# Mixture-of-experts layer: x in two loads of four experts, and the last weight but one in a single load

## The chip, the core and the metric

The kernel runs on one core of a Trainium2 chip. The metric is the device time of one execution in microseconds (us), as the median of five runs. A profile of one execution stands beside it.

## What is computed

Eight experts each have 256 rows of x, a first weight and a second weight; all inputs and the output are float32.

```python
# x: (8, 256, 512)   w1: (8, 512, 2048)   w2: (8, 2048, 512)
h = np.matmul(x, w1)
h = np.maximum(h, 0)
return np.matmul(h, w2).astype(np.float32)
```

Each w1[e] and each w2[e] is 4.19 MB in float32, so the sixteen weights are 67.1 MB; x is 4.19 MB and the output 4.19 MB.

## The kernel before

The matrix products run in bfloat16. The weights are loaded by GpSimd's DMA queue, which casts float32 to bfloat16 on the way; a weight tile holds 2048 KB after the cast, with 16 KB (32 KB before the cast) in each of the 128 partitions. `w1` and `w2` tiles each have three buffers (`WB = 3`), so `load_w1(3)` may start only when expert 0's first layer has read its weight, and so on. The queue works in the order of issue, and the order of the program is written out by hand (`manual_schedule`).

`first_layer(e)` makes the hidden layer of one expert: 16 blocks of 128 hidden units, each from four matmuls that contract over the 512 inputs, 64 matmuls of 128x256 in all. Four blocks share a PSUM tile, and ScalarE and VectorE take turns to apply relu and write `ht` as bfloat16. `second_layer(e)` makes 32 matmuls of 128x512, which alternate between the two row blocks and go through the 16 row groups (kt) of w2 in order; VectorE copies one result to `o_sb` and ScalarE the other.

x must have its inputs on the partitions, so it is transposed on TensorE (`transpose_x`, line 87), eight 128x128 blocks to a PSUM tile, and copied from there to `xt` by VectorE (line 100) or ScalarE (line 98). x comes in groups (`GROUPS`): experts 0 and 1 each by a float32 transfer of SyncE into `x_f`, cast by ScalarE (lines 155 and 156); experts 2 and 3 by one casting transfer of GpSimd, and experts 4 to 7 by another (line 65), in the midst of the weights. In `x_rows`, a group of n experts gives each partition 2n rows of 2 KB that lie one after the other in memory: 4 KB for one expert, 8 KB for two, 16 KB for four. The transposes of experts 1 and 2-3 stand between layers; those of experts 4-7 between the parts of `first_layer(2)`.

At the end the order is different: the first layers of experts 5, 6 and 7 run ahead of the second layers of 5, 6 and 7. The second weight of expert 6 comes in two halves of 8 row groups, that of expert 7 in 9 and 7, so that a second layer can start on the first piece (`load_w2`, lines 71 to 75). The results of experts 0 to 4 are stored by GpSimd's queue behind the last weight (`store(0, 5)`); those of expert 5 by five SyncE transfers (lines 191 and 192) while the last weight still arrives; those of experts 6 and 7 by a last SyncE transfer (line 194).

Of the kernel before, what the change touches and what calls it, by code (L numbers as in the profile page):

```python
# [10 lines left out]
def kernel(  # L11
# [7 lines left out]
    nc = tc.nc  # L19
    P = 128  # L20
    bf = mybir.dt.bfloat16
    f32 = mybir.dt.float32
    relu = mybir.ActivationFunctionType.Relu

    E, C, H = x.shape
    F = w1.shape[2]
    MT = C // P
    KT1 = H // P
    KT2 = F // P
# [1 line left out]
    WB = 3  # L31


    GROUPS = ((0, 1), (1, 1), (2, 2), (4, 4))


    w1_r = w1.rearrange("e (p kt) n -> e p kt n", p=P)
# [3 lines left out]
    const = ctx.enter_context(tc.tile_pool(name="const", bufs=1))  # L41
# [7 lines left out]

    w1_sb, w2_sb, ht = {}, {}, {}  # L50
    group_of = {e: g for g, (e0, n) in enumerate(GROUPS) for e in range(e0, e0 + n)}
    x_f = const.tile([P, 2, MT, H], f32, name="x_f")
    x_b = [const.tile([P, n * MT, H], bf, name=f"x_b{g}") for g, (_, n) in enumerate(GROUPS)]
    xt = [const.tile([P, KT1, MT, n * P], bf, name=f"xt{g}") for g, (_, n) in enumerate(GROUPS)]
    o_sb = const.tile([P, E, MT, H], f32, name="out_sb")
    identity = const.tile([P, P], bf, name="identity")

    def x_rows(g):
        e0, n = GROUPS[g]
        return x[e0:e0 + n].rearrange("e c k -> (e c) k").rearrange(  # L60
            "(p j) k -> p j k", p=P
        )

    def load_x(g):
        nc.gpsimd.dma_start(x_b[g][:], x_rows(g))  # L65

    def load_w1(e):
        w1_sb[e] = wpool.tile([P, KT1, F], bf, tag="w1", name="w1_sb")
        nc.gpsimd.dma_start(w1_sb[e][:], w1_r[e])  # L69

    def load_w2(e):
        w2_sb[e] = wpool.tile([P, KT2, H], bf, tag="w2", name="w2_sb")
        cuts = {E - 2: (0, 8, 16), E - 1: (0, 9, 16)}.get(e, (0, KT2))
        for lo, hi in zip(cuts, cuts[1:]):
            nc.gpsimd.dma_start(w2_sb[e][:, lo:hi, :], w2_r[e, :, lo:hi, :])  # L75

    def transpose_x(g, blocks=None):


        n = GROUPS[g][1]  # L80
        J = n * MT
        KB = 8 // J
        for b in blocks if blocks is not None else range(KT1 // KB):
            pt = ps_o.tile([P, KB, J, P], bf, tag="ps_o", name="pt_tr")
            for i in range(KB):
                for j in range(J):
                    nc.tensor.transpose(  # L87
                        pt[:, i, j, :], x_b[g][:, j, b * KB + i::KT1], identity[:]
                    )
            for i in range(KB) if n > 1 else (slice(0, KB),):  # L90
                if n > 1:
                    src = pt[:, i].rearrange("p (l m) q -> p l m q", m=MT)
                    dst = xt[g][:, b * KB + i].rearrange("p m (q l) -> p l m q", l=n)
                    flip = b * KB + i
                else:
                    src, dst, flip = pt[:, i], xt[g][:], g
                if flip % 2:
                    nc.scalar.copy(dst, src)  # L98
                else:
                    nc.vector.tensor_copy(dst, src)  # L100

    def first_layer(e, between=()):
        g = group_of[e]
        i0 = (e - GROUPS[g][0]) * P
        ht[e] = hpool.tile([P, KT2, C], bf, tag="ht", name="ht_sb")
        for q in range(KT2 // FB):
            ph = ps_h.tile([P, FB, C], f32, tag="ps_h", name="pt_h")
            for i in range(FB):
                for kt in range(KT1):
                    nc.tensor.matmul(  # L110
                        ph[:, i, :],
                        w1_sb[e][:, kt, FB * q + i::KT2],
                        xt[g][:, kt, :, i0:i0 + P],
                        start=(kt == 0),
                        stop=(kt == KT1 - 1),
                    )
            if q % 2:
                nc.vector.tensor_relu(ht[e][:, FB * q:FB * (q + 1), :], ph[:])  # L118
            else:
                nc.scalar.activation(ht[e][:, FB * q:FB * (q + 1), :], ph[:], relu)  # L120
            if between:
                between.pop(0)()

    def second_layer(e):
        po = [
            ps_o.tile([P, H], f32, tag="ps_o", name=f"pt_o{mt}") for mt in range(MT)
        ]
        for kt in range(KT2):
            for mt in range(MT):
                nc.tensor.matmul(  # L130
                    po[mt][:],
                    ht[e][:, kt, mt * P:(mt + 1) * P],
                    w2_sb[e][:, kt, :],
                    start=(kt == 0),
                    stop=(kt == KT2 - 1),
                )
        nc.vector.tensor_copy(o_sb[:, e, 0, :], po[0][:])  # L137
        nc.scalar.copy(o_sb[:, e, 1, :], po[1][:])  # L138
# [2 lines left out]
        nc.gpsimd.dma_start(out_r[:, e0:e1], o_sb[:, e0:e1])  # L141


    for e in (0, 1):
        nc.sync.dma_start(x_f[:, e], x_rows(e))
    load_w1(0)
    make_identity(nc, identity)
    load_w2(0)
    load_x(2)
    load_w1(1)  # L150
    load_w2(1)
    load_x(3)
    load_w1(2)
    load_w2(2)
    nc.scalar.copy(x_b[0][:], x_f[:, 0])  # L155
    nc.scalar.copy(x_b[1][:], x_f[:, 1])  # L156
    transpose_x(0)

    first_layer(0)
    load_w1(3)  # L160
    transpose_x(1)
    second_layer(0)
    load_w2(3)
    first_layer(1)
    load_w1(4)
    transpose_x(2)
    second_layer(1)
    load_w2(4)
    first_layer(2, [lambda kt=kt: transpose_x(3, [kt]) for kt in range(KT1)])
    load_w1(5)  # L170
    second_layer(2)
    first_layer(3)
# [52 lines left out]
```

## Time and profile before

| | us |
|---|---|
| median of five runs | 181.71 (181.46 to 181.98) |
| the profiled execution's own time | 181.98 |
| its span, first to last instruction | 180.2 |
| TensorE matmuls busy | 129.2 |
| VectorE busy | 31.8 |
| ScalarE busy | 31.6 |
| GpSimd busy | 12.3 |

The DMA queues moved 40.47 MB as they are counted at the destination, at a mean of 225 GB/s; HBM was read for 71.30 MB and written for 4.19 MB, 419 GB/s over the span. A casting load counts its 2 bytes per value at the destination and reads 4, so a stretch of pure weight loading shows about half the GB/s of a stretch of float32 stores at the same read or write rate. In the row of DMA shares, 9 means that the 16 DMA engines were busy for 90% or more of that fortieth of the span (4.5 us). PE is TensorE, DVE is VectorE, ACT is ScalarE, POOL is GpSimd, SP is SyncE; L130 is line 130 of the kernel.

### The profile page before, as it was taken

To read this page: it belongs to the slowest core of one execution; us is meant where nothing else is said; L and a number is where in the kernel's file an instruction comes from. 1 tells how busy PE (TensorE), PEld (TensorE's weight loads), DVE (VectorE), ACT (ScalarE), POOL (GpSimd) and SP (SyncE) were. 2 spreads that over 40 slices of the span, in tenths; PEclk is the share of its full clock that TensorE was granted. 3 is DMA by queue.
4 is the path that set the end of the run, shared out by engine and by line. 5 is a ranking of instruction groups with operands and counts; after the bars stand their busy time and mean duration, and the time that the engine had idled before them with its cause. 6 is when DMAs were issued, how large, how long until landed. Compare 5 with 4: busy or idle time off the path is not lost.

```text
span 180.2 us, 1823 instructions
## 1 busy us (share of the span) xinstructions
PE 129.2 (72%) x825; PEld 89.8 (50%) x832; DVE 31.8 (18%) x29; ACT 31.6 (18%) x32; POOL 12.3 (7%) x27
## 2 busy tenths in 40 slices
PE   0206999059993199988769794979494967999650
PEld 0105974048841189638624691349394953444220
DVE  0100220101411017610500122012222140011010
ACT  3300240102221026612200230012122220011010
POOL 7300010100101000100100004030000000000000
PEclk9999999956999759999969998799999996999995
DMA  5998999999899999989998999999899999999995
GB/s 220 246 233 185 222 233 211 196 233 225 182 233 233 211 196 233 229 185 225 233 225 182 233 229 204 207 233 225 185 229 233 211 196 211 226 209 223 312 416 230
DMA packets 4262, 40.47 MB, mean 225 GB/s; under 512 B 416, under 2 KB 416, under 8 KB 1952
## 3 DMA queue, kind: packets, MB, share of 16 engines
q0 software_dynamic: 3536, 37.75, 95.7%
q1 hardware_dynamic: 720, 2.62, 3.8%
q8 instruction: 6, 0.10, 0.2%
HBM read 71.30 MB, written 4.19 MB: 419 GB/s over the span
## 4 chain that ended last, share of the span: by engine, by line
DMA 44%; PE 41%; another core or an unknown queue 8%; issue 1%; POOL 1%; ACT 0%; POOLq 0%
DMA w_sb<-in_w_dram 44%; PE pt_o L130 21%; PE pt_h L110 19%; PE pt_tr L87 2%; ACT out_sb L138 0%; POOL x_b L65 0%; POOL w_sb L75 0%; POOL identity masks.py:199 0%; POOL identity masks.py:197 0%; POOL w_sb L69 0%; POOLq L209 0%
## 5 line engine op out<-in xcount | busy, mean ns | idle before, releaser
L110 PE MATMUL pt_h<-xt,w_sb 128*128 128x256 bf16 x512 | 64.9, 292 | 29.8 <-DMA w_sb<-in_w_dram 29.8
L110 PEld LDWEIGHTS <-w_sb 128*128 128x128 bf16 x512 | 59.5, 147 | 35.8 <-DMA w_sb<-in_w_dram 33.0
L130 PE MATMUL pt_o<-w_sb,ht_sb 128*128 128x512 bf16 x249 | 60.6, 400 | 9.7 <-DMA w_sb<-in_w_dram 8.9
L130 PEld LDWEIGHTS <-ht_sb 128*128 128x128 bf16 x256 | 26.0, 102 | 42.4 <-issue 16.0
L118 DVE TENSOR_SCALAR ht_sb<-pt_h 128x1024 bf16<-128x1024 f32 x16 | 19.7, 1228 | 64.6 <-PE pt_h L110 64.6
L120 ACT ACTIVATE ht_sb<-pt_h 128x1024 bf16<-128x1024 f32 x16 | 16.5, 1029 | 67.6 <-PE pt_h L110 67.6
L138 ACT COPY out_sb<-pt_o 128x512 f32<-128x512 f32 x8 | 4.7, 585 | 65.1 <-PE pt_o L130 65.1
L137 DVE COPY out_sb<-pt_o 128x512 f32<-128x512 f32 x8 | 5.5, 692 | 59.8 <-PE pt_o L130 59.8
L100 DVE COPY xt<-pt_tr 128x1024 bf16<-128x1024 bf16 (+1 forms) x5 | 7.1, 1439 | 18.1 <-PE pt_tr L87 18.1
L69 POOL DMA_DIRECT2D w_sb<-in_w_dram x8 | 4.4, 554 | 85.8 <-PE pt_h L110 85.0
L87 PE MATMUL pt_tr<-identity,x_b 128*128 128x128 bf16 x64 | 5.6, 243 | 5.1 <-ACT x_b L155 5.1
L98 ACT COPY xt<-pt_tr 128x1024 bf16<-128x1024 bf16 (+1 forms) x5 | 7.4, 1498 | 7.1 <-PE pt_tr L87 4.5
L87 PEld LDWEIGHTS <-x_b 128*128 128x128 bf16 x64 | 5.0, 122 | 5.2 <-ACT x_b L155 5.1
L75 POOL DMA_DIRECT2D w_sb<-in_w_dram x10 | 5.4, 547 | 23.3 <-PE pt_o L130 23.3
L155 ACT ACT_TABLE_LOAD x1 | 1.3, 1283 | 0.7 <-PEq L209 0.7
L155 ACT CAST x_b<-x_f 128x1024 bf16<-128x1024 f32 x1 | 1.0, 1045 | 2.0 <-DMA x_f<-in_x_dram 2.0
L65 POOL DMA_DIRECT2D x_b<-in_x_dram x2 | 1.1, 552 | 0.0
L156 ACT CAST x_b<-x_f 128x1024 bf16<-128x1024 f32 x1 | 1.0, 1046 | 0.2 <-DMA x_f<-in_x_dram 0.2
L141 POOL DMA_DIRECT2D out_dram<-out_sb x1 | 0.9, 866 | 0.1
masks.py:199 POOL TENSOR_SCALAR_AFFINE_SELECT identity<-identity 128x128 bf16<-128x128 bf16 x1 | 0.3, 288 | 0.1
masks.py:197 POOL MEMSET identity<- 128x128 bf16 x1 | 0.2, 223 | 0.0
L209 POOL MEMSET const-float32-0.0<- 128x1 f32 x1 | 0.1, 98 | 0.2 <-issue 0.2
(3 smaller groups left out, 0.3 us busy)
## 6 DMA issues: line engine op xcount, KB each, us to landing
w_sb<-in_w_dram POOLq DMA_DIRECT2D x14, 2048.0 KB, 45.2
out_dram<-out_sb POOLq DMA_DIRECT2D x1, 2560.0 KB, 55.8
w_sb<-in_w_dram POOLq DMA_DIRECT2D x2, 1024.0 KB, 46.9
w_sb<-in_w_dram POOLq DMA_DIRECT2D x1, 1152.0 KB, 45.2
x_f<-in_x_dram SPq DMA_DIRECT2D x2, 512.0 KB, 3.7
x_b<-in_x_dram POOLq DMA_DIRECT2D x1, 1024.0 KB, 47.9
out_dram<-out_sb SPq DMA_DIRECT2D x1, 1024.0 KB, 4.9
w_sb<-in_w_dram POOLq DMA_DIRECT2D x1, 896.0 KB, 50.2
```

What stands on the lines that cost most here:

```text
L69: nc.gpsimd.dma_start(w1_sb[e][:], w1_r[e])
L75: nc.gpsimd.dma_start(w2_sb[e][:, lo:hi, :], w2_r[e, :, lo:hi, :])
L87: nc.tensor.transpose(pt[:, i, j, :], x_b[g][:, j, b * KB + i::KT1], identity[:])
L98: nc.scalar.copy(dst, src)
L100: nc.vector.tensor_copy(dst, src)
L110: nc.tensor.matmul(ph[:, i, :], w1_sb[e][:, kt, FB * q + i::KT2], xt[g][:, kt, :, i0:i0 + P], start=(kt == 0), stop=(kt == KT1 - 1),)
L118: nc.vector.tensor_relu(ht[e][:, FB * q:FB * (q + 1), :], ph[:])
L120: nc.scalar.activation(ht[e][:, FB * q:FB * (q + 1), :], ph[:], relu)
L130: nc.tensor.matmul(po[mt][:], ht[e][:, kt, mt * P:(mt + 1) * P], w2_sb[e][:, kt, :], start=(kt == 0), stop=(kt == KT2 - 1),)
L137: nc.vector.tensor_copy(o_sb[:, e, 0, :], po[0][:])
L138: nc.scalar.copy(o_sb[:, e, 1, :], po[1][:])
L155: nc.scalar.copy(x_b[0][:], x_f[:, 0])
```

## The change

x now comes in two groups of four experts. The first is one float32 transfer of SyncE (2 MB, 16 KB in each partition), issued before the first weight; VectorE and ScalarE cast it in four pieces, two each, and all of its 32 transposes stand ahead of `first_layer(0)`. The second group is the same as the last of the four groups before. The casting transfer for experts 2 and 3 is gone, and the transposes of experts 1 and 2-3 no longer stand between layers. The second weight of expert 6 comes in one transfer; that of expert 7 is still cut.

```diff
-    GROUPS = ((0, 1), (1, 1), (2, 2), (4, 4))
+    GROUPS = ((0, 4), (4, 4))
...
-    x_f = const.tile([P, 2, MT, H], f32, name="x_f")
+    x_f = const.tile([P, 4 * MT, H], f32, name="x_f")
...
-        cuts = {E - 2: (0, 8, 16), E - 1: (0, 9, 16)}.get(e, (0, KT2))
+        cuts = (0, 9, 16) if e == E - 1 else (0, KT2)
...
-    for e in (0, 1):
-        nc.sync.dma_start(x_f[:, e], x_rows(e))
+    nc.sync.dma_start(x_f[:], x_rows(0))
     load_w1(0)
     make_identity(nc, identity)
     load_w2(0)
-    load_x(2)
     load_w1(1)
     load_w2(1)
-    load_x(3)
+    load_x(1)
     load_w1(2)
     load_w2(2)
-    nc.scalar.copy(x_b[0][:], x_f[:, 0])
-    nc.scalar.copy(x_b[1][:], x_f[:, 1])
+    for j in range(0, 4 * MT, 2):
+        if j % 4:
+            nc.scalar.copy(x_b[0][:, j:j + 2], x_f[:, j:j + 2])
+        else:
+            nc.vector.tensor_copy(x_b[0][:, j:j + 2], x_f[:, j:j + 2])
     transpose_x(0)
 
     first_layer(0)
     load_w1(3)
-    transpose_x(1)
     second_layer(0)
     load_w2(3)
     first_layer(1)
     load_w1(4)
-    transpose_x(2)
     second_layer(1)
     load_w2(4)
-    first_layer(2, [lambda kt=kt: transpose_x(3, [kt]) for kt in range(KT1)])
+    first_layer(2, [lambda kt=kt: transpose_x(1, [kt]) for kt in range(KT1)])
```

## The prediction

> **What bounds the kernel now.** I read the slices of the page first, then the chain of waits, the landings of the loads and the end of the span. The page's slices show DMA at eight tenths or more from the second slice to the last but one, while TensorE has gaps everywhere.
>
> ```profile
> PE   0206999059993199988769794979494967999650
> DMA  5998999999899999989998999999899999999995
> ```
>
> TensorE's waits name the loads. In the list of waits, the first line below is eight first layers that each waited for their weight:
>
> ```profile
> PE pt_h L110 <- DMA w_sb<-in_w_dram: 29.8, 8, 8.9
> PE pt_o L130 <- DMA w_sb<-in_w_dram: 8.9, 4, 2.5
> POOL w_sb L69 <- PE pt_h L110: 85.0, 5, 18.8
> ```
>
> The third line is GpSimd waiting for buffers, up to 18.8 us, and yet the DMA engines do not run dry, because loads are issued far ahead: 45.2 us from issue to landing in the median. So the kernel is one stream of transfers, and its length sets the time. Its unit is one weight. In the timeline, layers that wait for a weight start at 81.69, 91.40, 101.05, 110.73, 120.42, 130.16, 139.81 and 149.49: seven weights in 67.80 us, 9.69 each, or 433 GB/s of reading.
>
> The end follows the stream. The chain in order of time closes so:
>
> ```profile
> 165.08 4.06 PE pt_o L130 x18
> 169.14 1.39 another core or an unknown queue
> 170.53 0.04 issue
> 170.57 3.19 PE pt_o L130 x14
> ```
>
> TensorE has 18 matmuls on the first piece of the last weight, waits 1.39 for the second piece (issued 120.3, 50.2 to landing), does 14 more; the copies and the last store (4.9 us) follow. **What shortens the stream shortens the kernel; what delays TensorE costs nothing until 1.39 us are used up at this place.**
>
> **The x loads.** The timeline of GpSimd gives the issues, and the DMA issues the time to landing (last column):
>
> ```profile
> 2.44 0.55 POOL L75 DMA_DIRECT2D w_sb<-in_w_dram  x1
> 2.98 0.54 POOL L65 DMA_DIRECT2D x_b<-in_x_dram  x1
> 3.51 0.55 POOL L69 DMA_DIRECT2D w_sb<-in_w_dram  x1
> ```
> ```profile
> w_sb<-in_w_dram POOLq DMA_DIRECT2D x1, 2048.0 KB, 22.3
> ...
> x_b<-in_x_dram POOLq DMA_DIRECT2D x1, 512.0 KB, 24.3
> ...
> w_sb<-in_w_dram POOLq DMA_DIRECT2D x1, 2048.0 KB, 34.4
> ...
> x_b<-in_x_dram POOLq DMA_DIRECT2D x1, 1024.0 KB, 47.9
> ```
>
> The first second-layer weight lands at 24.74, the load of experts 2-3 (8 KB rows, 1.05 MB read) at 27.28: it takes 2.54. The load of experts 4-7 (16 KB rows, 2.10 MB) is issued at 4.55 and lands at 52.45, behind a weight of 47.53: 4.92. The two float32 loads of SyncE show in the start of the stream; columns are DMA share and GB/s at the end:
>
> ```profile
> 1.50:2.00 0.50, 0.00 (x0) 0.00 (x0) 0.00 (x0) 0.50 (x1) 0.50 (x2) 1.00 0.78 147
> 2.00:2.50 0.50, 0.00 (x0) 0.00 (x0) 0.00 (x0) 0.02 (x1) 0.42 (x3) 1.00 0.43 156
> 3.00:3.50 0.50, 0.00 (x0) 0.00 (x0) 0.00 (x0) 0.00 (x0) 0.50 (x1) 1.00 1.00 410
> ```
>
> Between 2.0 and 2.5 there is a lull, 57% of 0.5 us = 0.29. From 2.5 to 4.5 the rate is 410 to 426, mean 418: 1.05 MB take 2.51. So x of experts 0 to 3 holds the stream for 2.51 + 0.29 + 2.54 = **5.34** before.
>
> After, the same 2.10 MB come in one transfer. Its nearest row is the load of experts 4-7, with the same bytes read and the same 16 KB rows: 4.92. It differs in that it writes float32, so the other bound is the rate of the SyncE loads, 2.10 MB at 418 GB/s = 5.02. The lull may stay (0.29) or go, since a 16 KB row keeps an engine busy four times as long as a 4 KB row; the trace has no such start, and I take half, 0.15. Together 4.92 + 0.15 = 5.07, between 4.92 and 5.31: a **gain of 0.27 (0.03 to 0.42)**. The first weight, 2.4 us later, and everything up to the old place of experts 2-3 move back; behind that place they move forward.
>
> **The second weight of expert 6.** Its halves are issued at 109.61 and 110.15 and land at 154.3 (44.7 later) and 159.25 (49.1, since the two have a median of 46.9); the weight ahead lands at 149.48. So it takes 9.77 in two pieces against 9.69: **gain 0.08 (0 to 0.1)**.
>
> On TensorE this takes cover away. The second layer of expert 6 now begins when the whole weight has landed, about 159.2 on the old clock, and not at 157.9:
>
> ```profile
> 147.00:149.49 2.49, 0.01 (x1) 0.00 (x0) 1.23 (x1) 0.00 (x0) 0.00 (x0) 0.94 0.82 171
> 149.49:152.59 3.10, 2.88 (x7) 1.17 (x8) 0.00 (x0) 0.00 (x0) 0.00 (x0) 0.50 1.02 214
> 152.59:157.90 5.31, 5.31 (x26) 2.35 (x24) 0.01 (x1) 0.00 (x0) 0.00 (x0) 1.00 1.04 216
> 157.90:164.80 6.90, 6.85 (x32) 3.04 (x31) 0.68 (x2) 0.59 (x1) 0.00 (x0) 1.00 1.03 221
> ```
>
> Its 32 matmuls (6.90) end at 166.15 instead of 164.8, the next 18 (4.06) at 170.2, and the last piece lands at 170.5. The 1.39 of waiting shrink to about 0.3, so I count nothing for it, on 0.3 us of cover.
>
> **Everything else is hidden.** GpSimd loses two issues (0.54 each) and SyncE one (0.4); all loads behind them are queued tens of us ahead. The waits on GpSimd's remaining issues are still for the buffers' last readers. The 32 transposes now ahead of the first layer cost most if x arrives late. The 448 KB store of SyncE took 10.7 us among the weights against about 1.1 alone at 418 GB/s, so a SyncE transfer can be held up by weight packets. At worst x lands together with the first weight, at 15.07 + 2.42 = 17.5. Then come casts: ScalarE's take 1.05 each; the two on VectorE are not in the trace (0.69 to 2.55 by its copies, I take 1.23 as its relu, so 2.5 together). Transposes took 1.04 for eight at first, 4.2 for 32; the last copy takes 2.56. The first layer would start at 26.8 instead of 15.07, and lasts 9.3; the second, 7.1, ends at 43.2; expert 1 needs 9.8 and 7.1 and is done at 60.1, before its successor's weight lands at 62.3. Loads issued late (24.68 becomes 36) still join a queue that is full until the third second-layer weight, past 70. If VectorE's casts take 2.55 the chain is 2.6 later and still within a microsecond of 62.3, with 1.09 to 2.5 of waiting at each layer after it.
>
> **The sum.** 0.27 + 0.08 = 0.35. The profiled execution took 181.98, 1.78 more than its span, so 181.63 for one like it; the median of the runs is 0.27 lower, so 181.71 - 0.35 = **181.36**.
>
> The Trainium skill, "DMA: Bandwidth & Descriptors" (Anatomy of one DMA), gives a DMA about 2.0 us of fixed cost beside bytes at 436 GB/s; three DMAs fewer would then be worth 6 us, an estimate of 175.7. Seven weights 9.69 apart, with 4.19 MB in each, leave no room for such a cost between queued transfers, and the halves of expert 6's weight show 0.08.
>
> **Rivals.**
>
> *Slower: TensorE's clock falls in the new gap.* Of five waits of 2.4 to 2.6 us in the timeline (from 88.9, 108.3, 127.6, 137.4, 147.0), three were followed by half clock: 0.50 above, means of 0.84 and 0.82 in the stretches 91.40:101.05 and 110.73:120.42; two were not (1.00, 0.98). Three waits of 1.0 to 1.15 (80.6, 99.9, 119.4) were not. Expert 5's second layer takes 8.4 after a fall and 6.9 without one. With the fall it ends at 157.9, the gap is 1.3, and nothing happens. Without it (2 in 5) it ends at 156.4 and the gap is 2.8; a fall then (3 in 5) makes 3.1 us or more at half clock fall on expert 6, 1.55 lost, less 0.3 of cover: 1.25 on the end, so 182.6. That is 2/5 x 3/5 = 24% of executions; a median of five shows it in about 1 of 10 if executions differ at random and in 1 of 4 if they repeat. It decides from 0.3 us of delay on. I give it 19%.
>
> "TensorE: Matmul & The Clock Gate" of the skill (Part 1) halves the clock after an idle window of about 3.4 us, which by itself would spare both gaps and leave 181.36; the row of 0.50 after 2.49 us of idle differs, and the row decides.
>
> *No change: the lull stays and float32 packets keep 418 GB/s.* Then x gains 0.03 and the cut up to 0.08: 181.6. For it: nothing shows that longer rows shorten the lull. 16%.
>
> *Much faster: the slowest engine loses less.* The weight behind experts 2-3 took 10.63 (27.28 to 37.91), 0.94 too much, and in 26:34 the profile has one instruction packet of 0.8% of 16 engines, 1.0 us. If such packets fell so that the engine ending last is spared, 0.9 more would go: 180.5. Against it: as many instructions are fetched as before. 8%.
>
> *x late beyond the cover.* It would take a first layer some 12 us later than my worst case. 2%, at 182.5.
>
> The forecast has 55%. About 0.2% (0.36 us) is what a measurement of this kernel can tell from no change, and 0.35 lies on that edge.
>
> **How the numbers follow.** Faster: a little over half of the forecast's 0.55 (0.29), all of the much faster case (0.08), and 0.03 of the no-change case, whose cut gains its part: 0.40. Slower: clock 0.19, late x 0.02, and 0.02 each of the forecast and the no-change case, for covers that prove too thin: 0.25. The rest is the same: 0.35. The forecast's own range is 181.2 to 181.7; up to 182.5 it takes in most of the slower cases, and down to 180.9 a part of the faster one.
>
> **What would show it.** Right: weights still 9.7 apart; experts 4-7's load landing 0.2 to 0.4 earlier; expert 6's second layer waiting for its weight; a wait of about 0.3 before the last 14 matmuls. Wrong: no wait there, with a clock near 0.5 in expert 6's second layer; a longer lull at the start of the stream; TensorE still busy with older layers when weights land, past 62.

## The result and the profile after

The changed kernel is slower. Its median is 182.03 us (181.66 to 183.26, 29 runs), against 181.64 (181.28 to 182.18, 53 runs) for the kernel before in the same comparisons; the ratio is 1.0031, with a 95% interval of 1.0023 to 1.0039. The forecast was 181.36: the range held the time, but the sign was wrong.

The 29 times are not one group. Sixteen lie between 181.66 and 182.10 (median 181.92), thirteen between 182.44 and 183.26 (median 182.55), and none between. Those of before are one group. So two things are to be explained: why the lower group lies 0.28 above before instead of 0.35 below, and what makes the upper group.

The two spans hide both. The profiled execution of after took 181.87 and is of the lower group; that of before took 181.98, near the top of its own; their spans are 180.1 and 180.2. Stages must be compared here. On the page of after, the DMA engines are as busy as before and SyncE's load takes 12.5 us from issue to landing (3.7 before):

```profile
DMA  6999999999999999999999999999999999999995
...
x_f<-in_x_dram SPq DMA_DIRECT2D x1, 2048.0 KB, 12.5
```

The start of the stream of after in the same half microseconds that the prediction showed; the last two columns are the share of the DMA engines and GB/s:

```profile
1.50:2.00 0.50, 0.00 (x0) 0.00 (x0) 0.00 (x0) 0.50 (x1) 0.50 (x2) 1.00 2.08 393
2.00:2.50 0.50, 0.00 (x0) 0.00 (x0) 0.00 (x0) 0.02 (x1) 0.42 (x3) 1.00 0.41 66
3.00:3.50 0.50, 0.00 (x0) 0.00 (x0) 0.00 (x0) 0.00 (x0) 0.50 (x2) 1.00 0.46 197
```

Before, the rate was 410 by 3.0 us; here it is 197. (A packet counts where it begins, so the 393 of the first line are long packets just begun, and a stretch of 3 us is safer to compare than one of half a microsecond.) The lull did not shrink with longer rows, it became longer. The first weight (issued 1.25, 16.8 to landing) lands at 18.05.

The end of after, from the chain in order of time:

```profile
159.53 0.04 issue
159.57 4.26 PE pt_o L130 x19
163.84 0.05 issue
163.89 9.81 PE pt_o L130 x44
```

Expert 6's second layer starts when its weight has landed, as forecast, and then TensorE works to 173.70 without a wait. The wait of 0.3 us that was to remain ahead of the last 14 matmuls is not there. The timeline of TensorE shows why this execution is of the lower group: the clock fell ahead of expert 5's second layer (8.75 instead of 7.1), so that the wait behind it is short and expert 6's second layer runs at full speed:

```profile
149.91 8.75 PE L130 MATMUL pt_o<-w_sb,ht_sb 128*128 128x512 bf16 x31 [2.50 <-DMA w_sb<-in_w_dram]
159.57 14.11 PE L130 MATMUL pt_o<-w_sb,ht_sb 128*128 128x512 bf16 x63 [0.91 <-DMA w_sb<-in_w_dram]
```

### The profile page after: what moved, and what is told of

It is laid out like the page before. It is cut to its first block, busy times and chain, and to the rows that moved or that the text cites. A ratio compares the mean times of both kernels' runs of the same rounds, so it can differ in the third digit from the quotient of the medians.

```text
span 180.1 us, 1820 instructions
## 1 busy us (share of the span) xinstructions
PE 128.4 (71%) x825; PEld 89.5 (50%) x832; DVE 35.9 (20%) x30; ACT 33.9 (19%) x31; POOL 11.2 (6%) x25
## 4 chain that ended last, share of the span: by engine, by line
DMA 52%; PE 35%; another core or an unknown queue 6%; POOL 2%; issue 1%; ACT 0%; POOLq 0%
DMA w_sb<-in_w_dram 52%; PE pt_o L130 20%; PE pt_h L110 14%; PE pt_tr L87 1%; POOL w_sb L69 1%; POOL w_sb L75 1%; ACT out_sb L138 0%; POOL identity masks.py:199 0%; POOL identity masks.py:197 0%; POOLq masks.py:199 0%; POOLq L208 0%
## 5 line engine op out<-in xcount | busy, mean ns | idle before, releaser
L110 PE MATMUL pt_h<-xt,w_sb 128*128 128x256 bf16 x512 | 64.4, 289 | 21.2 <-DMA w_sb<-in_w_dram 18.5
L130 PE MATMUL pt_o<-w_sb,ht_sb 128*128 128x512 bf16 x249 | 59.5, 395 | 9.8 <-DMA w_sb<-in_w_dram 9.3
L87 PE MATMUL pt_tr<-identity,x_b 128*128 128x128 bf16 x64 | 6.0, 254 | 14.4 <-DVE x_b L157 14.1
L87 PEld LDWEIGHTS <-x_b 128*128 128x128 bf16 x64 | 5.1, 124 | 14.9 <-DVE x_b L157 14.1
L100 DVE COPY xt<-pt_tr 128x1024 bf16<-128x1024 bf16 x4 | 9.9, 2518 | 11.1 <-PE pt_tr L87 11.1
L98 ACT COPY xt<-pt_tr 128x1024 bf16<-128x1024 bf16 x4 | 9.7, 2497 | 4.0 <-PE pt_tr L87 4.0
L69 POOL DMA_DIRECT2D w_sb<-in_w_dram x8 | 4.4, 554 | 83.6 <-PE pt_h L110 82.8
L75 POOL DMA_DIRECT2D w_sb<-in_w_dram x9 | 4.9, 543 | 25.2 <-PE pt_o L130 25.2
L157 DVE CAST x_b<-x_f 128x1024 bf16<-128x1024 f32 x2 | 1.3, 690 | 13.3 <-DMA x_f<-in_x_dram 13.3
L65 POOL DMA_DIRECT2D x_b<-in_x_dram x1 | 0.6, 558 | 0.0
## 6 DMA issues: line engine op xcount, KB each, us to landing
x_f<-in_x_dram SPq DMA_DIRECT2D x1, 2048.0 KB, 12.5
```

The source lines that it names most:

```text
L87: nc.tensor.transpose(pt[:, i, j, :], x_b[g][:, j, b * KB + i::KT1], identity[:])
L110: nc.tensor.matmul(ph[:, i, :], w1_sb[e][:, kt, FB * q + i::KT2], xt[g][:, kt, :, i0:i0 + P], start=(kt == 0), stop=(kt == KT1 - 1),)
L130: nc.tensor.matmul(po[mt][:], ht[e][:, kt, mt * P:(mt + 1) * P], w2_sb[e][:, kt, :], start=(kt == 0), stop=(kt == KT2 - 1),)
```

## Experiments: one half of the change at a time

The theories: **G**, the gap before expert 6's second layer lets the clock fall and makes the upper group; **S**, the slow start of SyncE's load costs the rest.

**The whole weight alone.** The kernel before, with this edit:

```diff
-        cuts = {E - 2: (0, 8, 16), E - 1: (0, 9, 16)}.get(e, (0, KT2))
+        cuts = (0, 9, 16) if e == E - 1 else (0, KT2)
```

> The kernel before, with one edit: the second weight of expert 6 comes whole. Theory G (the gap): the second layer of expert 6 now waits about 1.1 to 2.7 us for its weight; where the clock falls in the gap, about 4 executions of 10, the end comes 0.7 to 1.2 us later, and in the others the time is that of before. So two groups of times, one within 0.15 of before and one 0.7 to 1.2 above, median of the change between 0 and +0.4 us. Theory S (the start alone costs the time): one group of times, 0 to 0.1 below before.

Measured: median 182.00, ratio 1.0014 (1.0005 to 1.0024). The 11 times fall into two groups, four from 181.44 to 181.66 and seven from 181.95 to 182.16. The profiled execution is one of the upper group. Its matmuls in the timeline, and the end in stretches (granted clock, DMA share and GB/s are the last three columns):

```profile
149.36 7.07 PE L130 MATMUL pt_o<-w_sb,ht_sb 128*128 128x512 bf16 x32 [0.94 <-DMA w_sb<-in_w_dram]
159.04 15.66 PE L130 MATMUL pt_o<-w_sb,ht_sb 128*128 128x512 bf16 x64 [2.62 <-DMA w_sb<-in_w_dram]
```
```profile
159.04:160.00 0.96, 0.96 (x5) 0.48 (x5) 0.00 (x0) 0.00 (x0) 0.00 (x0) 0.99 0.96 202
160.00:163.40 3.40, 3.40 (x10) 1.21 (x9) 0.00 (x0) 0.00 (x0) 0.00 (x0) 0.50 0.99 222
163.40:174.72 11.32, 11.30 (x53) 4.90 (x50) 0.89 (x2) 0.59 (x1) 0.00 (x0) 1.00 1.02 328
```

This is the clock rival of the prediction, step by step: expert 5's second layer ran at full clock (7.07), a wait of 2.62 followed, and a microsecond after its end the clock fell to 0.50 for 3.4 us. The 64 matmuls take 15.66, against 14.1 in after's profile. The groups are 0.4 to 0.5 apart and not 0.7 to 1.2; that is taken up below.

**Work in the gap.** The changed kernel, with extra matmuls in the two waits:

```diff
-    for e in (5, 6):
-        second_layer(e)
+    def keep_busy(n):
+        spare = ps_h.tile([P, FB, C], f32, tag="ps_h", name="pt_spare")
+        for _ in range(n):
+            nc.tensor.matmul(
+                spare[:, 0:2, :], identity[:], x_b[1][:, 0, :], start=True, stop=True
+            )
+
+    keep_busy(5)
+    second_layer(5)
+    keep_busy(6)
+    second_layer(6)
```

> The changed kernel, with 5 extra matmuls of 128x512 on TensorE before the second layer of expert 5 and 6 before that of expert 6; their results are not used. They stand in the waits for the weights (1.1 and 1.3 us of them), so that no wait there is longer than 1.5 us. Theory G with the clock as its cause: the clock is 1.00 in the second layers of experts 5 and 6, the upper group of times (182.4 and above) is gone, and the median is 0.1 to 0.3 below the changed kernel. Rival (the wait itself makes the upper group, or the loads do, whatever the clock): the two groups stay as they are, at 4 of 10 above 182.4.

Measured: median 181.94 (181.83 to 182.15, 11 runs), one group; the upper one is gone. TensorE's timeline shows the waits cut to 1.4 and 1.3 us and both layers at full clock:

```profile
147.51 1.24 PE L190 MATMUL pt_spare<-x_b,identity 128*128 128x512 bf16 x5
150.19 7.07 PE L130 MATMUL pt_o<-w_sb,ht_sb 128*128 128x512 bf16 x32 [1.44 <-DMA w_sb<-in_w_dram]
157.09 1.46 PE L190 MATMUL pt_spare<-x_b,identity 128*128 128x512 bf16 x6
159.84 14.13 PE L130 MATMUL pt_o<-w_sb,ht_sb 128*128 128x512 bf16 x64 [1.28 <-DMA w_sb<-in_w_dram]
```

The loads and the wait for the whole weight are as they were, and only TensorE's idling is less. So the upper group is made by the clock. What is left, 181.94, is the lower group of after (181.92).

**Both together on the x of before.** The whole weight, with the same extra matmuls, on the kernel before:

> The kernel before with the second weight of expert 6 whole, and 5 and 6 extra matmuls (results unused) in the waits before the second layers of experts 5 and 6. Theory G with the clock: the upper group of the run with the whole weight alone (181.95 to 182.16) is gone, all times lie at 181.4 to 181.7, and the median is 0 to 0.1 below before, the prediction's term for one transfer less. Rival (the wait for the whole weight costs the time without the clock): the times stay near 182.0.

Measured: 181.64 (181.45 to 181.93, 11 runs), ratio 1.0001 (0.9992 to 1.0010). One group, at the time of before. The forecast gain of 0.08 for one transfer less is within the interval and can't be told from nothing. This was the candidate for a version that beats both; it only equals the kernel before.

**The x part alone.** The changed kernel, with the halves of expert 6's weight restored (the diff above, reversed):

> The changed kernel, with the second weight of expert 6 in two halves again. Theory G: one group of times, since no gap is left before the second layer of expert 6; the median is that of before, or 0.2 below it by the row of experts 4-7's load. Theory S (the first 16 KB packets of SyncE's load start slowly and nothing hides it): one group, 0.3 to 0.5 us above before, with the first weight landing at about 18.1 and a lull between 2.0 and 4.0 us in the share of the DMA engines.

Measured: 181.97 (181.79 to 182.22, 11 runs), one group, ratio 1.0018 (1.0009 to 1.0026), so 0.33 above before. The first weight lands at 18.1 (1.24 and 16.9). Theory S holds, and the two parts add: 0.18% and 0.14%, each to about 0.09, are 0.32%, against 0.31% for the whole change.

## Experiments: why the start is slow

**Shorter rows, same bytes.** The changed kernel with four SyncE transfers:

```diff
-    nc.sync.dma_start(x_f[:], x_rows(0))
+    for j in range(0, 4 * MT, 2):
+        nc.sync.dma_start(x_f[:, j:j + 2], x_rows(0)[:, j:j + 2])
```

> The changed kernel, with x of experts 0 to 3 in four SyncE transfers of 4 KB rows instead of one of 16 KB rows; the bytes, the casts and all else are the same. Theory S: the lull at the start is that of before (one half us, 0.43 busy), the first weight lands 0.4 to 0.6 earlier than the changed kernel's 18.1, and all times are 0.3 to 0.5 below those of the changed kernel, still in two groups. Rival (the size of the load or its place ahead of the first weight costs the time, not its rows): the first weight lands at 18.0 to 18.2 as in the changed kernel, and the times do not move.

Measured: 183.30 (182.88 to 183.65, 6 runs). Both readings fail. The rows are 4 KB as in before, and the start is slower still. Each line here is the stretch from 1.5 to 4.5 us, in which only SyncE's loads move data, first of before, then of this run:

```profile
1.50:4.50 3.00, 0.00 (x0) 0.00 (x0) 0.00 (x0) 0.99 (x2) 2.92 (x7) 1.00 0.88 329
```
```profile
1.50:4.50 3.00, 0.00 (x0) 0.00 (x0) 0.00 (x0) 0.51 (x1) 2.92 (x7) 1.00 0.81 229
```

After has 273, the x part alone 268, the run with work in the gap 279; the two runs so far with the x of before have 314 and 307. So the length of a row is not it. What after and this run share is that the first transfer's rows, one per partition, lie 16 KB apart, over 2 MB of memory; before, each of its transfers covers 512 KB without a break. That is theory **A**.

The run also shows how far the order of x may slip. The later pieces came among the weights' packets, and ScalarE waited up to 21.4 us for one of them; the first layer began at 32.7, and TensorE came to expert 2's first layer only at 64.5, past the landing of its weight (63.0). The first weight itself lands at 17.4, earlier than after's, because two of the four pieces land only at 17.6 and 28.6. TensorE waited for a weight again at 82.5; what share of this run's time the late x cost, the run alone does not say.

**Cut by partitions.** The x part alone, with its load in four pieces of 32 partitions, 512 KB each without a break:

```diff
-    nc.sync.dma_start(x_f[:], x_rows(0))
+    for p in range(0, P, 32):
+        nc.sync.dma_start(x_f[p:p + 32], x_rows(0)[p:p + 32])
```

> The run with the x change alone (one 2 MB load in 16 KB rows), with that load cut by partitions into four SyncE transfers of 32 rows of 16 KB, each of 512 KB that lie together in memory; the bytes and the row length are the same. Theory A (the first packets are slow because they touch 2 MB of memory at once): the DMA engines move 310 GB/s or more between 1.5 and 4.5 us, against 268 with one load and 329 before, the first weight lands 0.3 to 0.5 earlier than 18.16, and the median falls by 0.3. Rival R (16 KB rows are slow at the start, or any 2 MB float32 load ahead of the weight is): 265 to 280 GB/s, first weight at 18.1 to 18.2, median unchanged at 181.97.

Measured: 184.90 (184.66 to 184.96, 4 runs); the first weight lands at 21.2. As a test of A it fails, since the cut brings a larger cost of its own. These are the stretches from 2.5 us in which SyncE's load runs alone, of this run and of before:

```profile
2.50:6.50 4.00, 0.00 (x0) 0.00 (x0) 0.00 (x0) 0.00 (x0) 3.14 (x6) 1.00 1.01 209
```
```profile
2.50:4.50 2.00, 0.00 (x0) 0.00 (x0) 0.00 (x0) 0.47 (x1) 2.00 (x4) 1.00 1.02 418
```

With only 32 partitions written at a time the rate is half, 209 against 418, while the engines count as busy. Neither the length of the rows nor the place of the bytes explains it: later packets of after, 16 KB too, run at full rate with 128 partitions (0.61 us each against 1.27 here), and 512 KB in one piece is what before loads.

**One transfer over 1 MB.** The kernel before, with x of experts 0 and 1 in one SyncE transfer (`GROUPS = ((0, 2), (2, 2), (4, 4))`, rows of 8 KB):

> The kernel before, with x of experts 0 and 1 in one SyncE transfer of 1 MB in 8 KB rows instead of two of 512 KB in 4 KB rows; bytes, queue and place are the same, and all else is as before. Theory A: the first packets touch 1 MB instead of 512 KB, so the rate between 1.5 and 4.5 us falls below before's 314 to 329, to 290 to 310 GB/s, and the first weight lands 0.1 to 0.3 later than 15.07. Rival R by row length: about half of the loss of 16 KB rows, 290 to 310 too; this run alone does not part A from R by rows, but it parts both from a third reading, that only the second megabyte on SyncE costs, which expects 314 to 329 and 15.0 to 15.1.

```profile
1.50:4.50 3.00, 0.00 (x0) 0.00 (x0) 0.00 (x0) 0.51 (x1) 2.92 (x7) 1.00 0.85 284
```

Measured: 284 GB/s, a first weight at 15.3 (15.04 before), and a median of 181.75, ratio 1.0009 (1.0000 to 1.0017). The same megabyte on the same queue starts more slowly because of its shape alone. (The median says little of it: in the profiled execution, 181.90, the clock also fell ahead of the last second layer, which took 8.8.)

**Four transfers, each in one place.** The kernel before, with x of experts 2 and 3 on SyncE too, one transfer of 512 KB for each expert:

```diff
-    GROUPS = ((0, 1), (1, 1), (2, 2), (4, 4))
+    GROUPS = ((0, 1), (1, 1), (2, 1), (3, 1), (4, 4))
...
-    for e in (0, 1):
+    for e in range(4):
         nc.sync.dma_start(x_f[:, e], x_rows(e))
...
+    nc.scalar.copy(x_b[2][:], x_f[:, 2])
+    nc.scalar.copy(x_b[3][:], x_f[:, 3])
...
```

> The kernel before, with x of experts 2 and 3 loaded as experts 0 and 1 are: by SyncE in float32, 512 KB each that lie together in memory, 4 KB rows; the casting load of GpSimd for them is gone, and ScalarE casts them ahead of their transposes. SyncE thus loads the same 2 MB as in the run of four SyncE transfers of 4 KB rows, in as many transfers with as long rows; only the memory that each transfer spans differs, 512 KB against 2 MB. Theory A (the lull comes from the span of memory that the first packets touch): 305 to 330 GB/s between 1.5 and 4.5 us, as before (329, 314, 307) and not 229; the stream then loses 0.2 to 0.4 to small packets that alternate with those of the weights, and the median is 0.1 to 0.4 above before. Rival (any 2 MB of float32 on SyncE ahead of the first weight makes the lull): 229 to 280 GB/s.

```profile
1.50:4.50 3.00, 0.00 (x0) 0.00 (x0) 0.00 (x0) 0.88 (x2) 2.92 (x7) 1.00 0.87 325
```

Measured: 325 GB/s, so the slow start is gone with the same bytes, rows and number of transfers as in the run that had 229. The landings agree: the first two weights come at 16.6 and 27.65, against 17.4 and 28.5 in that run. Theory A is shown as far as these runs go: the start is slow where the first transfer takes its rows from a wide stretch of memory. In all of them the spacing of the rows (4, 8 or 16 KB) and the whole stretch (512 KB, 1 or 2 MB) change together, so which of the two counts, and what in the memory or on the way makes it so, no run shows.

The median is 182.04 (181.96 to 182.36, 11 runs), ratio 1.0023 (1.0014 to 1.0032), and still no better than the large load. SyncE's third and fourth transfers now alternate with the weights' packets: its loads take up to 26.4 us to land. I expected a loss of 0.1 to 0.4 from that, but most of the 0.43 measured has another place: the end of the program. These are SyncE's semaphore instructions from 178.5 us on, first of before, then of this run:

```profile
L220 SPq EVENT_SEMAPHORE  x3: 17/17/28, 179.3 to 180.1; - x3
```
```profile
L222 SPq EVENT_SEMAPHORE  x9: 17/28/28, 179.0 to 180.2; - x9
```

The last store lands at 179.0 here and at 179.3 in the profile of before, but the span ends 1.27 after the landing instead of 0.89, because six more of these instructions, 0.06 apart, follow it. The three runs with four SyncE loads of x all have 1.26 to 1.27 at this place, the nine others 0.89 to 0.91; why these instructions stand behind the store there, the traces do not say. So about 0.37 of the 0.43 is this tail, and 0.06 is left for the stream, too little to tell from nothing. 2 MB of x on SyncE lose here either way, in one transfer by the start and in four by the tail.

## Experiments: what a late end costs

The clock's fall took 1.5 us from expert 6's second layer (15.66 against 14.1) and yet the groups are only 0.4 to 0.65 apart. Two runs of the kernel before, with extra matmuls ahead of the last second layer, ask where the rest goes:

```diff
+    spare = ps_h.tile([P, FB, C], f32, tag="ps_h", name="pt_spare")
+    for _ in range(13):
+        nc.tensor.matmul(
+            spare[:, 0:2, :], identity[:], x_b[3][:, 0, :], start=True, stop=True
+        )
     second_layer(7)
```

The second run has `range(20)` in place of `range(13)`.

> The kernel before, with 13 extra matmuls of 128x512 (results unused, 2.8 us at full clock) ahead of the second layer of expert 7, so that its end comes about 1.4 us later than the last weight alone allows. The prediction's rule (the last store follows the last matmul at a fixed 4.9 us): the median rises by 1.3 to 1.5 us. The other reading (the last store shares the engines with the store of experts 0 to 4, and starts later among fewer packets): the last store takes 3.9 to 4.2 us instead of 4.9, and the median rises by 0.4 to 0.8.

Measured: 181.55 (181.46 to 182.13, 11 runs), ratio 1.0003 (0.9992 to 1.0013). The profiled execution shows why it does not decide: the clock stayed up in expert 5's second layer, the extra matmuls filled time in which TensorE would have waited, and the last matmul ended at 173.3. The delay was too small, so 20 were put there:

> The run before this one with 20 extra matmuls (4.3 us at full clock) instead of 13 ahead of the second layer of expert 7. The second layer of expert 6 ends at 163.4 where the clock stays up and at 164.8 where it falls before expert 5, so the last matmul ends 0.9 or 2.4 us later than before. The prediction's rule (the last store lands a fixed 4.9 us after its issue): two groups of times, 0.9 and 2.4 above before. The other reading (the store has fewer packets beside it the later it starts, down to some 3.9 us): 0 to 0.3 and 1.2 to 1.6 above before, and a last store of 3.8 to 4.2 us in the profile.

Measured: median 182.00, nine times from 181.89 to 182.14 and three from 183.47 to 183.60 (12 runs; ratio 1.0039, 1.0015 to 1.0064). In this comparison one of 17 executions of the kernel before took 182.75, the only such time of it on record; it has no profile. The profiled execution is of the lower group (181.89). Its chain, its last store, and the stretch in which the store of experts 0 to 4 comes to its end, beside the same stretch of before:

```profile
163.32 4.32 PE pt_spare L195 x20
167.64 3.67 PE pt_o L130 x17
171.31 0.05 issue
171.36 3.20 PE pt_o L130 x14
```
```profile
out_dram<-out_sb SPq DMA_DIRECT2D x1, 1024.0 KB, 4.0
```
```profile
175.60:176.40 0.80, 0.00 (x0) 0.00 (x0) 0.00 (x0) 0.00 (x0) 0.00 (x0) 1.00 0.46 184
```
```profile
175.60:176.40 0.80, 0.00 (x0) 0.00 (x0) 0.00 (x0) 0.00 (x0) 0.00 (x0) 1.00 1.01 415
```

The matmuls end at 174.56. The last weight landed at 170.0 there, so without the extra work they could have ended at 173.2: 1.3 us of delay, and the lower group lies 0.3 above before. The two profiles say the same: with 20 the last store is issued 1.22 later than with 13 (175.19 and 173.97) and lands 0.39 later, and the execution took 0.39 more. Before, the last store shares full engines with the store of experts 0 to 4 (415 GB/s) and takes 4.9; issued later it has fewer packets beside it and takes 4.0, and the engines run half empty meanwhile (184 GB/s). So the last store gives back 0.8 to 0.9 us of a late end. The upper group is 1.6 to 1.7 above the lower. It has no profile; if the fall ahead of expert 5's second layer makes it (some 1.4 later at the end, by the recorded expectation), then past that cover delay costs in full, which is argued and not shown.

## Why the prediction was wrong, step by step

- **What bounds the kernel**: right. Weights still land 9.7 apart in every profile, and what moved the time were the start of the stream and the last microseconds.
- **The x loads**: the step that gave the sign. I put the lull at half of 0.29, because a 16 KB row keeps an engine busy four times as long. By 17.58 the kernel before has both its first weight and the load of experts 2-3 (15.04 + 2.54); the sum had the first weight of after at 17.31, a gain of 0.27; it landed at 18.05, and at 18.14 in the run with x alone. The term is a loss of 0.47 to 0.56. The sign to look for, the load of experts 4-7 landing 0.2 to 0.4 earlier, did not come: 52.56 against 52.46. The bound was wrong, not only the choice: I took the old lull as the most that could stay, though it was measured on loads of 512 KB that lie together and the new load spans 2 MB, and the reason for a smaller one, that a 16 KB row keeps an engine busy longer, was taken from no row of this kind.
- Of that loss 0.33 reach the end in the run with x alone. Which later stage gives back the other 0.1 to 0.2 is open.
- **The whole weight of expert 6**: the gain of 0.08 is not to be told from nothing (ratio 1.0001). The 0.3 us of cover behind it, on which I counted nothing, were too thin: 0.2 are left in the profile of the run with work in the gap on the x of before, none in after's. I had read the cover off one execution, of 181.98, near the top of its group: there the last piece landed 11.32 behind expert 6's whole weight, and TensorE needs some 10.95 for the 50 matmuls between; in the other eleven profiles it lands 10.84 to 11.18 behind.
- **The clock rival**: right in mechanism, wrong in both sizes. I gave it 24% of executions and 1.25 us; it is 13 of 29 and 0.63 us (182.55 less 181.92). The frequency came from one profile: three of five waits were followed by half clock, so I let the clock fall ahead of expert 5's second layer in 3 of 5 executions, each wait by itself. But the waits hang together: a layer at half clock ends late and leaves a short wait behind it. Of the ten profiles with no extra matmuls ahead of that layer the clock fell there in four. In four of the other six it had fallen one layer earlier, and the wait ahead of expert 5 was only 0.8 to 0.94. So expert 5's second layer ran at full clock in 6 of 10 and not in 2 of 5; 6/10 x 3/5 is 36%; if the upper group of the run with 20 extra matmuls, 3 of 12, is that fall, 9/12 x 3/5 is 45%. After had 13 of 29, the whole weight alone 7 of 11. Both are estimates made afterwards, and few executions stand behind them. The price left out the 0.8 to 0.9 us that the last store gives back.
- The rule of the Trainium skill that I set beside this row ("TensorE: Matmul & The Clock Gate", Part 1) says that the window of activity is free-running. The two groups, of one and the same program, agree with that. The length it gives, about 3.4 us of idling, does not: the clock fell after a wait of 2.62, and in two other profiles after waits of 1.95 and 1.98.
- **Late x**: hidden, as worked out. After's first layer began as its weight landed (the first recorded matmul is at 18.35) and ran freely from 21.4, and the run of four 4 KB pieces, whose first layer began at 32.7, waited for a weight again at 82.5.
- **The fixed cost of a DMA** by the skill's page would have been a gain of 6 us (an estimate; the page gives that cost for GpSimd's path, and one of the three transfers is SyncE's); the whole change lost 0.4.

## What to carry to other kernels

Price a first load by the memory that its first packets span as well as by its bytes and rows; a lull measured on one shape is no bound for another. Where an execution can go two ways, ask the spread of many times, not one profile, how often each happens. Before a delay at the end is priced, look at what the last transfer shares the engines with: a late start may be given back, up to the point where the engines run empty. And read what stands behind the last transfer too: there, not in the stream, the runs with four loads of x lost 0.37 us.

## What the runs showed of the hardware

- A SyncE load of 128 rows that lie 16 KB apart ran at 229 to 279 GB/s from 1.5 to 4.5 us (four kernels, a profile of each); loads of 512 KB in one piece ran at 307 to 329 (six kernels).
- Loads that write 32 partitions at a time ran at 209 GB/s, half of the 418 of loads over 128 partitions, with the engines counted as busy.
- A SyncE transfer that starts among casting loads can wait long: 512 KB took up to 26.4 us to land, and 3.4 alone. That engines take packets of the queues in turn is what the skill's "DMA: Bandwidth & Descriptors" says (Queues, rings and completion order), and these landings agree.
